# A sliding-window copy: half-size staging transfers, a first batch half loaded in two channel parts, and a first tile filled in two channel ranges

## The chip, the cores and the metric

The kernel runs on one core of a Trainium2 chip. The metric is device time in microseconds for one execution; the median of three runs of the kernel before is 185.81 us (185.74 to 185.81).

## The reference

The input `x` has 16 batches, 64 channels and 64 x 64 pixels, all float32 (16.78 MB). The output has, for each batch and each of 15 x 15 window places, all 64 channels of an 8 x 8 window; windows step by 4, so neighbours overlap by half. Nothing is calculated:

```python
for i in range(n_h):
    for j in range(n_w):
        result[:, i, j] = x[:, :, 4*i:4*i+8, 4*j:4*j+8]
```

The output is 3600 rows of 4096 floats (16 KB each, 58.98 MB). So each input pixel is read once and written nearly four times.

## The kernel before, in words

**Layout.** The image is cut in height into four quarters of 16 rows (`HQ`), the channels into two halves of 32 (`CH`, here ch0 and ch1), the batch into two halves of eight (`NY`, here y=0 and y=1). The tile `Lt` holds the whole input: a partition is one (channel half, batch, height quarter), with 32 channels of 16 x 64 pixels. ch0 sits on partitions 0 to 63, ch1 on 64 to 127, and in each the first 32 partitions are y=0.

**Two ways in.** The first eight channels of each half (`FC` = 8) are *staged*: eight transfers of 512 KB (L118, four on ScalarE's queue, four on SyncE's) put them into the output buffers `GG`, which are not in use yet, and 16 copies (L137, n % 3 == 0 on ScalarE, the others on VectorE) bring them to `Lt`. A staging transfer writes 16 partitions, and reads DRAM in pieces of 4 KB (one channel, 16 rows). The other 24 channels of each half go straight into `Lt` (L61, called at L126 to L128): for each y and height quarter q, SyncE loads 22 channels of ch0 (for the first six of the eight (y, q) cut in two transfers of 10 and 12), GpSimd (POOL) loads the remaining two channels of ch0 (64 KB) and then all 24 of ch1 (768 KB). Each direct load writes eight partitions. ScalarE and SyncE together have eight transfers in flight before an issue waits for an earlier one to land, and POOL has eight of its own: the ninth and later issues each carry a wait on the semaphore of the transfer eight before.

**Tiles out.** `GG` is four output buffers (`G[0]` to `G[3]`) of 128 partitions x 16 KB. There are 31 tiles. A tile is filled by copies out of `Lt` and then stored; tile n goes into buffer n % 4, so its fill waits until tile n-4 has been stored. Stores of the first 29 tiles are indirect transfers from POOL (L149), behind POOL's loads in the same queue; the last two are issued by SyncE (L258). I number the tiles from 0.

- Tiles 0, 1 and 2 are `part(0, j)` (L200): eight copies of 32 partitions x 2048 elements (L208; n % 3 == 0 on ScalarE, the others on VectorE). They need y=0 alone.
- Then `unit(j, 0)` (64-partition copies, L169) and `part(1, j)` alternate: tiles 3 to 8. They need y=1 too. Tile 4 and tile 8 are both `part(1, j)` in `G[0]`.
- Tiles 9 to 28 are mostly "cross" units, three for each plain one; in these VectorE does two plain shuffles (L179) and two shifting shuffles (L172). A cross tile has 112 rows to store.
- The last two tiles (L256) are the last window column.

Order on each engine is the order of the program: all copies out of the staging first, then tile 0, 1, and so on.

Of the kernel before, what the change touches and what calls it, by code (L numbers as in the profile page):

```python
# [10 lines left out]
def kernel(  # L11
# [7 lines left out]
    nc = tc.nc  # L19
    P = nc.NUM_PARTITIONS  # L20

    B, C, H, W = x.shape
    Bo, NH, NW, Co, WSo, WSo2 = out.shape
    WS = int(window_size)
    ST = int(stride)
# [5 lines left out]
    CH = 2  # L31
    HQ = P // (B * CH)
    CL = C // CH
# [6 lines left out]
    NY = B // YB  # L40
    QP = YB * HQ
# [10 lines left out]
    L = Lt[:, :, 0 : RB * W].rearrange("p c (r w) -> p c r w", r=RB)  # L52
# [1 line left out]

    SMALL, SPLIT = 2, 6

    def load(eng, ch, y, q, c0, c1):
        p0 = ch * HP + y * QP + q  # L60
        eng.dma_start(out=L[p0 : p0 + QP - HQ + 1 : HQ, c0:c1, :, :], in_=x_v[ch, y, q, :, c0:c1, :])  # L61
# [49 lines left out]
    TC = GF // (RB * W)  # L111
    FC = NG * TC // CH
    S = [GG[:, ch * NG // CH : (ch + 1) * NG // CH].rearrange("p n f -> p (n f)").rearrange("p (c r w) -> p c r w", c=FC, r=RB) for ch in range(CH)]
    x_b = x.rearrange("b (ch cl) (hq r) w -> ch hq b cl (r w)", ch=CH, hq=HQ)
    for q in range(HQ):
        for ch in range(CH):
            s = S[ch][QP + q : QP + q + (B - 1) * HQ + 1 : HQ]
            (nc.scalar, nc.sync)[ch].dma_start(out=s, in_=x_b[ch, q, :, 0:FC, :])  # L118

    for y in range(NY):
        for q in range(HQ):
            mid = (FC + CL) // 2
            for c0, c1 in [(FC + SMALL, mid), (mid, CL)] if y * HQ + q < SPLIT else [(FC + SMALL, CL)]:
                load(nc.sync, 0, y, q, c0, c1)  # L126
            load(nc.gpsimd, 0, y, q, FC, FC + SMALL)
            load(nc.gpsimd, 1, y, q, FC, CL)  # L128

    PC = TC // 2  # L130
    first = [(0, ch, c) for ch in range(CH) for c in range(0, FC, PC)]
    then = [(1, ch, c) for ch in range(CH) for c in range(0, FC, PC)]
    for n, (y, ch, c) in enumerate(first + then):
        f = slice(QP + y * QP, QP + (y + 1) * QP)
        d = slice(ch * HP + y * QP, ch * HP + (y + 1) * QP)
        copy = nc.vector.tensor_copy if n % 3 else nc.scalar.copy
        tc.keep_in_program_order(copy(out=L[d, c : c + PC, :, :], in_=S[ch][f, c : c + PC]))  # L137
# [10 lines left out]
    def scatter(g, ix, j, s):  # L148
        st = nc.gpsimd.indirect_dma_start(  # L149
            out=o_v,  # L150
            out_offset=bass.IndirectOffsetOnAxis(ap=ix[:, 0:1], axis=0),
            in_=g.rearrange("p c r w -> p (c r w)"),
            in_offset=None,
            element_offset=(s * NW + j) * CFREE,
            bounds_check=B * NWIN - 1,
            oob_is_err=False,
        )
        free(st)
# [36 lines left out]
    def tile_():  # L195
        nonlocal at
        at += 1
        return G[(at - 1) % NG]

    def part(y, j):  # L200
        g = tile_()
        order = [(d, ch) for ch in range(CH) for d in range(P // QP)]
        for n, (d, ch) in enumerate(order):
            s, dj = d // NY, d % NY
            cols = slice((j + dj) * ST, (j + dj) * ST + WS)
            f = (ch * NY + y) * QP
            tc.keep_in_program_order(
                (act if n % 3 == 0 else dve)(  # L208
                    out=g[d * QP : (d + 1) * QP, ch * CL : (ch + 1) * CL, :, :],
                    in_=L[f : f + QP, :, s * ST : s * ST + WS, cols],  # L210
                )
            )
        scatter(g, (idx_y0, idx_y1)[y], j, 0)
# [16 lines left out]
            scatter(g, (idx_hi, idx_lo)[turn], j, s)  # L230

    for n in range(EARLY):
        part(0, 2 * n)
    plain = [(j, 0) for j in range(2 * EARLY, NW - 1)]
    cross = [(j, 2) for j in range(NW)]
    for n in range(EARLY):
        unit(*plain.pop(0), (dve, dve))
        part(1, 2 * n)
# [8 lines left out]
    j = NW - 1  # L247
    for s in range(2):
        g = tile_()
        cols = slice(j * ST, j * ST + WS)  # L250
        for y in range(NY):
            d = slice(QP + y * QP, QP + (y + 1) * QP)
            for ch in range(CH):
                f = slice(ch * HP + y * QP, ch * HP + (y + 1) * QP)
# [39 lines left out]
```

## Time and profile before

| | us |
|---|---|
| median of three runs | 185.81 |
| the profiled execution | 185.77 |
| its span, first to last instruction | 184.0 |
| outside the span | 1.77 |
| VectorE busy (DVE) | 153.9 (84%) |
| ScalarE busy (ACT) | 150.6 (82%) |
| GpSimd busy (POOL) | 49.6 (27%) |
| first copy out of the staging | 17.6 |
| first copy of tile 0 | 29.9 |
| first store issued | 36.95 |
| last copy ends | 173.7 |

A window row gives a stretch of the span, its length, then each engine's busy time with the number of instructions, the granted clock, and last the mean busy share of the 16 DMA engines and the rate they moved. The share can be a little above 1, since a packet may begin before the one ahead of it on the same engine has ended. In a timeline row the first number is the start, the second the time from the start of the first instruction merged into the row to the end of the last, and the bracket at its end says how long the engine had been idle and what ended that.

### The profile page before, as it was taken

How to read it: one execution, taken by the hardware profiler on the slowest of the kernel's cores; microseconds unless marked ns; L12 is line 12 of the kernel's file. 1: busy time of each engine (PE TensorE's matmuls, PEld its weight loads, DVE VectorE, ACT ScalarE, POOL GpSimd, SP SyncE). 2: the span in 40 equal slices, each digit the busy share in tenths (PEclk: the TensorE clock that was granted, in tenths of full speed). 3: DMA queues.
4: the chain of work that ended last, by engine and by line, in shares of the span. 5: the costliest groups of instructions: out<-in, count | busy, mean ns of one | idle time of the engine just before them, and what ended most of it. 6: DMA issues, size and time to landing. Idle time of an engine off the chain costs nothing.

```text
span 184.0 us, 612 instructions
## 1 busy us (share of the span) xinstructions
DVE 153.9 (84%) x213; ACT 150.6 (82%) x100; POOL 49.6 (27%) x50
## 2 busy tenths in 40 slices
DVE  5001999999999897999999999999999999999700
ACT  0001999999999999999899999998979999899600
POOL 7500575033253434221121112111211121113000
DMA  5999999999999999999999999999999999999995
GB/s 157 398 411 407 411 412 409 413 410 444 422 431 435 424 442 417 447 424 431 431 426 435 427 438 427 431 424 431 422 420 427 427 427 403 435 417 406 420 431 232
DMA packets 10596, 75.80 MB, mean 412 GB/s; under 512 B 2896, under 2 KB 2896, under 8 KB 6992
## 3 DMA queue, kind: packets, MB, share of 16 engines
q0 software_dynamic: 7760, 63.71, 82.4%
q1 hardware_dynamic: 2256, 9.96, 13.3%
q10 hardware_dynamic: 576, 2.10, 3.1%
q14 instruction: 4, 0.03, 0.0%
HBM read 16.78 MB, written 62.91 MB: 433 GB/s over the span
## 4 chain that ended last, share of the span: by engine, by line
DVE 61%; DMA 21%; issue 10%; SPq 1%; DVEq 1%
DVE GG L179 24%; DVE GG L172 16%; DVE GG L208 15%; DMA GG<-in_x_dram 8%; DMA out_dram<-GG,idx_y 7%; DMA Lt<-in_x_dram 6%; DVE GG L256 3%; DVE GG L169 2%; SPq L118 1%; DVE GG L184 0%; DVEq L289 0%; DVEq L169 0%; DVEq L208 0%; DVEq L179 0%; DVEq L256 0%
## 5 line engine op out<-in xcount | busy, mean ns | idle before, releaser
L169 ACT COPY GG<-Lt 64x2048 f32<-64x2048 f32 x46 | 87.2, 1897 | 3.9 <-DMA out_dram<-GG,idx 1.2
L179 DVE STREAM_SHUFFLE GG<-Lt 64x1024 f32<-64x1024 f32 (+4 forms) x39 | 52.9, 1357 | 1.3
L208 DVE COPY GG<-Lt 32x2048 f32<-32x2048 f32 x30 | 36.6, 1218 | 2.7 <-DMA out_dram<-GG,idx_y 1.6
L172 DVE STREAM_SHUFFLE GG<-Lt 64x1024 f32<-64x1024 f32 x30 | 38.5, 1282 | 0.0
L208 ACT COPY GG<-Lt 32x2048 f32<-32x2048 f32 x18 | 34.1, 1897 | 0.4
L137 DVE COPY Lt<-GG 32x2048 f32<-32x2048 f32 x10 | 11.8, 1224 | 14.1 <-DMA GG<-in_x_dram 14.0
L61 POOL DMA_DIRECT2D Lt<-in_x_dram x16 | 14.1, 886 | 16.3 <-DMA Lt<-in_x_dram 15.7
L149 POOL DMA_INDIRECT out_dram<-GG,idx_y x6 | 10.1, 1690 | 27.6 <-DVE GG L208 27.6
L149 POOL DMA_INDIRECT out_dram<-GG,idx_lo x8 | 7.7, 966 | 30.2 <-DVE GG L172 18.9
L137 ACT ACT_TABLE_LOAD x1 | 1.3, 1283 | 17.6 <-DMA GG<-in_x_dram 17.6
L149 POOL DMA_INDIRECT out_dram<-GG,idx x8 | 10.6, 1321 | 18.1 <-DVE GG L179 13.3
L149 POOL DMA_INDIRECT out_dram<-GG,idx_hi x7 | 6.8, 966 | 26.5 <-DVE GG L172 18.9
L137 ACT COPY Lt<-GG 32x2048 f32<-32x2048 f32 x6 | 11.2, 1894 | 0.1
L183 ACT COPY GG<-Lt 64x256 f32<-64x256 f32 (+2 forms) x21 | 10.2, 484 | 0.5
L169 DVE COPY GG<-Lt 64x2048 f32<-64x2048 f32 x6 | 7.3, 1222 | 0.2
L256 ACT COPY GG<-Lt 32x768 f32<-32x768 f32 x8 | 6.6, 828 | 0.1
L256 DVE COPY GG<-Lt 32x1280 f32<-32x1280 f32 x8 | 6.5, 818 | 0.1
L75 DVE TENSOR_SCALAR tb<-pi 128x1 int32<-128x1 int32 x1 | 0.2, 154 | 1.0 <-POOL pi L72 1.0
L184 DVE COPY GG<-Lt 64x1280 f32<-64x1280 f32 x1 | 0.9, 875 | 0.0
L78 DVE TENSOR_SCALAR th<-tc 128x1 int32<-128x1 int32 x2 | 0.3, 154 | 0.0
L81 DVE TENSOR_TENSOR th<-tc,tq 128x1 int32<-128x1 int32 x2 | 0.3, 154 | 0.0
L179 DVE LOAD_MASK_SELECT GG<-Lt x39 | 0.3, 7 | 0.0
(21 smaller groups left out, 3.0 us busy)
## 6 DMA issues: line engine op xcount, KB each, us to landing
Lt<-in_x_dram POOLq DMA_DIRECT2D x8, 768.0 KB, 15.7
Lt<-in_x_dram SPq DMA_DIRECT2D x6, 384.0 KB
GG<-in_x_dram SPq DMA_DIRECT2D x4, 512.0 KB
GG<-in_x_dram ACTq DMA_DIRECT2D x4, 512.0 KB
out_dram<-GG SPq DMA_DIRECT2D x2, 1024.0 KB
Lt<-in_x_dram SPq DMA_DIRECT2D x6, 320.0 KB
Lt<-in_x_dram SPq DMA_DIRECT2D x2, 704.0 KB
Lt<-in_x_dram POOLq DMA_DIRECT2D x8, 64.0 KB, 15.2
```

The source lines that it names most:

```text
L61: eng.dma_start(out=L[p0 : p0 + QP - HQ + 1 : HQ, c0:c1, :, :], in_=x_v[ch, y, q, :, c0:c1, :])
L78: nc.vector.tensor_scalar(out=d[:, :], in0=a[:, :], scalar1=float(m), scalar2=None, op0=ALU.mult)
L118: (nc.scalar, nc.sync)[ch].dma_start(out=s, in_=x_b[ch, q, :, 0:FC, :])
L137: tc.keep_in_program_order(copy(out=L[d, c : c + PC, :, :], in_=S[ch][f, c : c + PC]))
L149: st = nc.gpsimd.indirect_dma_start(out=o_v, out_offset=bass.IndirectOffsetOnAxis(ap=ix[:, 0:1], axis=0), in_=g.rearrange("p c r w -> p (c ...
L169: copy(out=g[d, cs, :, :], in_=L[f, :, s * ST : s * ST + WS, cols])
L172: nc.vector.stream_shuffle(out=g[d, cs, ST:WS, :], in_=L[f, :, 0:ST, cols], mask=nxt)
L179: nc.vector.stream_shuffle(out=out, in_=in_, mask=same)
L183: act(out=out[:, 0:k], in_=in_[:, 0:k])
L184: other(out=out[:, k:], in_=in_[:, k:])
L208: (act if n % 3 == 0 else dve)(out=g[d * QP : (d + 1) * QP, ch * CL : (ch + 1) * CL, :, :], in_=L[f : f + QP, :, s * ST : s * ST + WS, cols],)
L256: copy(out=g[d, ch * CL + c0 : ch * CL + c1, :, :], in_=L[f, c0:c1, s * ST : s * ST + WS, cols])
```

## The change

The staging goes in two rounds of four channels: sixteen transfers of 256 KB in place of eight of 512 KB. The copies out of it are the same sixteen, in another order: first all of channels 0 to 3 (both y, both halves), then 4 to 7.

The direct loads of y=0 are cut at channel 20 (`MID`): first channels 8 to 19 for all four q, then 20 to 31 for all four q, then y=1 as before. In each of the three blocks POOL again loads two channels of ch0 and all of ch1, so it issues 24 loads in place of 16. SyncE still issues 14: 10 channels, 10 channels, and for y=1 the first two q cut in 10 and 12, the others whole.

Tile 0 is filled in two channel ranges, 0 to 19 for all eight partition pieces and then 20 to 31, in 16 copies in place of 8. All other tiles are as before.

```diff
-    SMALL, SPLIT = 2, 6
+    SMALL, SPLIT, MID = 2, 2, 20
...
-    for q in range(HQ):
-        for ch in range(CH):
-            s = S[ch][QP + q : QP + q + (B - 1) * HQ + 1 : HQ]
-            (nc.scalar, nc.sync)[ch].dma_start(out=s, in_=x_b[ch, q, :, 0:FC, :])
-    for y in range(NY):
+    for c in range(0, FC, TC):
         for q in range(HQ):
-            mid = (FC + CL) // 2
-            for c0, c1 in [(FC + SMALL, mid), (mid, CL)] if y * HQ + q < SPLIT else [(FC + SMALL, CL)]:
-                load(nc.sync, 0, y, q, c0, c1)
-            load(nc.gpsimd, 0, y, q, FC, FC + SMALL)
-            load(nc.gpsimd, 1, y, q, FC, CL)
+            for ch in range(CH):
+                s = S[ch][QP + q : QP + q + (B - 1) * HQ + 1 : HQ, c : c + TC]
+                (nc.scalar, nc.sync)[ch].dma_start(out=s, in_=x_b[ch, q, :, c : c + TC, :])
+    for y, c0, c1 in ((0, FC, MID), (0, MID, CL), (1, FC, CL)):
+        for q in range(HQ):
+            mid = (c0 + c1) // 2
+            for a, b in [(c0 + SMALL, mid), (mid, c1)] if y and q < SPLIT else [(c0 + SMALL, c1)]:
+                load(nc.sync, 0, y, q, a, b)
+            load(nc.gpsimd, 0, y, q, c0, c0 + SMALL)
+            load(nc.gpsimd, 1, y, q, c0, c1)
...
-    first = [(0, ch, c) for ch in range(CH) for c in range(0, FC, PC)]
-    then = [(1, ch, c) for ch in range(CH) for c in range(0, FC, PC)]
-    for n, (y, ch, c) in enumerate(first + then):
+    moves = [(y, ch, c + n) for c in range(0, FC, TC) for y in range(NY) for ch in range(CH) for n in range(0, TC, PC)]
+    for n, (y, ch, c) in enumerate(moves):
...
-    def part(y, j):
+    def part(y, j, ranges=((0, CL),)):
         g = tile_()
-        order = [(d, ch) for ch in range(CH) for d in range(P // QP)]
-        for n, (d, ch) in enumerate(order):
+        order = [(d, ch, c0, c1) for c0, c1 in ranges for ch in range(CH) for d in range(P // QP)]
+        for n, (d, ch, c0, c1) in enumerate(order):
...
-                    out=g[d * QP : (d + 1) * QP, ch * CL : (ch + 1) * CL, :, :],
-                    in_=L[f : f + QP, :, s * ST : s * ST + WS, cols],
+                    out=g[d * QP : (d + 1) * QP, ch * CL + c0 : ch * CL + c1, :, :],
+                    in_=L[f : f + QP, c0:c1, s * ST : s * ST + WS, cols],
...
-        part(0, 2 * n)
+        part(0, 2 * n, *([] if n else [((0, MID), (MID, CL))]))
```

## The prediction

> **What bounds the kernel now.** I read the page's slices first, then its queue lines, then a table of stretches, then the chain of waits, then the timeline of the engine that the chain names.
>
> The slices:
>
> ```profile
> DVE  5001999999999897999999999999999999999700
> ACT  0001999999999999999899999998979999899600
> POOL 7500575033253434221121112111211121113000
> DMA  5999999999999999999999999999999999999995
> ```
>
> Two things look full: the DMA engines from the first slice on, and VectorE (DVE) with ScalarE (ACT) from the fourth. Only one can be what the end waits for.
>
> ```profile
> core 0: us, DVE busy (x) ACT busy (x) POOL busy (x), PEclk, DMA share, GB/s
> 2.00:6.00 4.00, 1.42 (x11) 0.00 (x0) 4.00 (x8) 1.00 0.95 306
> 6.00:17.00 11.00, 0.00 (x0) 0.00 (x0) 0.94 (x2) 1.00 1.03 411
> 17.00:44.00 27.00, 25.61 (x22) 26.11 (x15) 11.32 (x9) 1.00 1.04 412
> 70.00:130.00 60.00, 58.93 (x88) 57.87 (x41) 13.53 (x13) 1.00 1.01 431
> 130.00:174.00 44.00, 43.06 (x64) 40.98 (x33) 8.76 (x9) 1.00 1.00 420
> 174.00:182.00 8.00, 0.00 (x0) 0.00 (x0) 0.00 (x0) 1.00 0.99 422
> ```
>
> From 6 to 17 us VectorE and ScalarE do nothing, and the DMA share is 1.03 all the same: the DMA engines don't miss them. From 17 to 44 it is 1.04, and after that about 1.0. So the transfers run back to back from 2.2 us (the first packet) to 182.2 (the last).
>
> ```profile
> DMA packets 10596, 75.80 MB, mean 412 GB/s; under 512 B 2896, under 2 KB 2896, under 8 KB 6992
> ## 3 DMA queue, kind: packets, MB, share of 16 engines
> q0 software_dynamic: 7760, 63.71, 82.4%
> q1 hardware_dynamic: 2256, 9.96, 13.3%
> q10 hardware_dynamic: 576, 2.10, 3.1%
> ```
>
> 82.4 + 13.3 + 3.1 = 98.8% of 184.0 us is 181.8 us of packet time on each of 16 engines, in a stretch of 180.0 us (packets overlap by about 1%). **The DMA work is the time.** By the trace's packet records a packet of 16 KB takes 611 to 616 ns, one of 4 KB 159, one of four bytes (a semaphore count or a filler) 9. The page gives 2896 of the last, 6992 - 2896 = 4096 of 4 KB (the input once) and 3604 larger ones, 3600 of them output rows.
>
> Is VectorE bound too? The chain and the timeline around 70 us answer:
>
> ```profile
> 58.06 11.98 DMA out_dram<-GG,idx_y
> 70.05 0.03 issue
> 70.09 0.04 issue
> 70.14 1.23 DVE GG L208
> ```
>
> ```profile
> 70.14 6.22 DVE L208 COPY GG<-Lt 32x2048 f32<-32x2048 f32 x5 [0.94 <-DMA out_dram<-GG,idx_y]
> ```
>
> VectorE stands still for 0.66 us up to 60.47 (tile 6) and, as this row shows, for 0.94 up to 70.14 (tile 8) until buffers are stored, the second time until tile 4's store, issued at 58.06, has landed at 70.05. That store waited in the queue behind tiles 0 to 3. So tile 8 begins when the DMA engines have finished all loads and five tiles, and nothing done earlier on VectorE moves that. From there VectorE has no further stop of note (58.93 of 60.00 us) and is a little slower than the stores: a cross tile is issued every 4.74 us and its 112 rows take 4.26 us. Its lead, from the end of an issue to the tile's first packet, falls from 5.2 us (tile 7) to 1.25 (tile 27). That is why the rate sinks from 431 to 420 GB/s after 130 us.
>
> **The change, part by part**, against the profiled execution (185.77 us, 0.04 under the median).
>
> *Bytes and large packets:* the same. Every channel still comes in 4 KB pieces: 4096 x 159 ns stay.
>
> *More transfers.* The page's 576 packets on q10 are four staging transfers of 128 pieces and 16 counts each. A SyncE direct load posts eight counts (2256 = 4 x 144 + 1408 pieces + 14 x 8 + two stores of 64 + 16): it runs on eight engines of the 16. A POOL load puts pieces on eight engines, a filler for each on the other eight, and 16 counts; with 16 counts for each of 29 stores and 240 skipped rows that gives the 2624 four-byte packets of q0. From 20 to 40 us q1 takes 7.4 engines (46.3% of 16) and q0 9.2: **SyncE's ch0 fills one half of the engines, POOL's ch1 the other.** Added now: 8 staging transfers x 16 counts = 128; 8 POOL loads x 16 counts = 128; 64 fillers for the eight more 64 KB loads. On an engine of the ch0 half that is 8 + 8 = 16 packets, on the other 8 + 8 + 8 = 24: 16 x 9 = 0.14 us and 24 x 9 = 0.22 us. The ch0 half is the later one (its loads end at 44.4 us, the other's at 43.9, and first stores start on the other at 43.2), so I take **+0.13 us**, bounds 0 (counts run beside data) and +0.22. The 64 fillers stay inside it.
>
> The Trainium skill (SBUF — State Buffer, The DMA setup-cost knee) gives every transfer a fixed cost of about 2 us, mostly completion, and speaks against this change. As an estimate by that page, 16 more transfers one after the other would be 32 us, to 218. The 1.03 from 6 to 17 us, under eight staging transfers and a queue behind each, shows such a cost hidden while the next transfer is queued.
>
> *The start.* From 2 to 6 us 306 GB/s x 4 us = 1.22 MB are moved, where 411 GB/s would be 1.64: 1.0 us is lost there, while the first transfers ramp up. With 256 KB each, the first eight hold 2.1 MB, about 5 us of work, and SyncE and ScalarE issue one each 0.6 to 0.8 us (L118: 3.06 us for four), which supplies 0.5 MB in 0.75 us, above what the engines take. The ninth waits for the first to land; six or seven are then still queued, so I take 0, bounds -0.3 (shorter first transfers land their data sooner) and +1.0 (the loss doubles with the number of hand-overs).
>
> *Copies out of the staging* begin when 2.1 MB instead of 4.2 have landed, at about 9 to 10 us instead of 17.6, and end near 22. *Tile 0* still needs the last y=0 loads of ch1, which now land near 30 (27.9 before: they queue behind more), so its store can go out near 33 instead of 36.95; the eight extra copies are smaller, 16 x 32 partitions, some 60 ns more each, all in front of a wait. *Tile 3* needs all loads, near 44.5. All this is **time at no price and no gain**: the first store's packets can't run before the loads are through (43.2 us now, 4.5 us after its issue ended), and tile 8 waits for tile 4's store as shown. Without the cover: tile 3 later than 56 us would stop the DMA; it is about 49.
>
> Sum: 185.77 + 0.13 + 0 = **185.90 us**.
>
> **Rivals.**
>
> *POOL can't feed its half (slower).* This is the mechanism of the other sign.
>
> ```profile
> 1.48 4.92 POOL L61 DMA_DIRECT2D Lt<-in_x_dram  x8 [0.52 <-issue]
> ...
> 22.22 2.76 POOL L61 DMA_DIRECT2D Lt<-in_x_dram  x2 [2.00 <-DMA Lt<-in_x_dram]
> ```
>
> Eight issues took 4.92 us before VectorE copied, 0.62 each; beside its copies a pair took 2.76, 1.38 each. Copies now start at 9.5 us, and 16 of the 24 loads fall beside them, so nearly all late issues are of the slow kind. A pair of 64 + 384 KB gives the ch1 half 384 KB / 206 GB/s = 1.9 us of work and costs POOL up to 2.8. Four such pairs must follow the first four: 4 x 0.9 = 3.6 us short. Against it: three pairs, 5.7 us, are queued when a wait ends, and the ch1 half is 1.2 us ahead. It decides once issue plus the way to the first packet passes 5.7 us: that way was at most 1.25 us at tile 27 (4.0 in all, safe) and 3.4 at the very first POOL load (6.2, not safe). Price: 3.6 - 1.2 = 2.4 at the worst, half of it likely: 187.1, from 186.2 to 188.3. The Trainium skill (SBUF — State Buffer, SBUF: two separate sides) says GpSimd can't write descriptors while VectorE copies float32 in its two-port mode; the rise from 0.62 to 1.38 agrees with it.
>
> *The start loses more (slower).* Twice as many hand-overs between short transfers: +0.4 to +1.0, 186.3 to 186.8. A fixed cost per transfer, as on the page named above, would show itself here.
>
> *The lead is larger to the end (faster).* Tiles 0 to 2 are filled some 4 us sooner. If that lead lived on, the 52 us after 130 us would run at 431 instead of 420 GB/s: 52 x 11/431 = 1.3 us, 184.6; half of it, 185.3. Against it stand the two stops at 60.47 and 70.14: a lead is taken back there.
>
> *It doesn't do what it says:* if the copies start no sooner (the second round of staging holds ScalarE's queue), the time is that of the main case, by the same argument.
>
> **How the numbers follow.** 0.2% is 0.37 us, about what a measurement of this kernel can tell from no change; "same" reaches from 185.44 to 186.18. Main case 0.57 (185.6 to 186.15), POOL's half 0.17, start 0.13, lead 0.10, something not seen on the slow side 0.03. The faster cases come to 0.11, the slower ones to 0.32 (a little of each lies inside the bound), same 0.57. The range reaches from half of the lead case to the middle of POOL's: 185.3 to 187.2.
>
> **What would show it.** Right: DMA share near 1.03 from 6 to 44 us with SyncE's and POOL's queues both full, copies from about 9.5 us, the stops of VectorE at tiles 6 and 8 longer than 0.66 and 0.94, tile 8 again beginning at 70.1 to 70.3, the rate after 130 us again near 420. POOL's rival: a stretch between 22 and 32 us with a share near 0.5 to 0.8. The start's: 2 to 6 us with less than 1.2 MB. The lead's: VectorE waiting for buffers after 80 us and 430 GB/s to the end. Wrong altogether if tile 4's store lands more than 0.4 us from 70.05 with the DMA share full, since then the packets themselves cost something else.

## The result, and the profile after

The changed kernel takes 187.13 us, median of six runs (186.87 to 187.52), beside 185.78 (185.68 to 185.83) for the kernel before: a ratio of 1.0072, 95% interval 1.0059 to 1.0085. That is 1.35 us, or 0.72%, slower. The profiled execution also took 187.13, with a span of 185.3 us (184.0 before). The time lies in the range given, at its upper end (187.2); the main case, 185.90, was 1.2 us too low.

The table of stretches of the kernel after, with the columns that the prediction showed:

```profile
2.00:6.00 4.00, 1.43 (x11) 0.00 (x0) 4.00 (x8) 1.00 0.94 295
6.00:17.00 11.00, 5.19 (x5) 4.71 (x3) 3.08 (x4) 1.00 0.99 364
17.00:44.00 27.00, 23.31 (x24) 23.99 (x17) 15.84 (x15) 1.00 1.03 410
70.00:130.00 60.00, 58.12 (x88) 57.17 (x39) 13.91 (x14) 1.00 1.01 430
130.00:174.00 44.00, 43.31 (x65) 41.76 (x35) 9.24 (x10) 1.00 1.00 422
```

Row by row against before: 6 to 17 us fell from 411 to 364 GB/s, which is 47 x 11 = 517 KB, or 1.26 us at 411. The rows on each side lost 11 x 4 KB and 2 x 27 KB, 0.1 us each. After the loads the rates are those of before (430 for 431, 422 for 420). So the load phase lost 1.5 us, and 0.2 came back at the end. The busy share hides this: it reads 0.99, and only the rate tells. In single microseconds:

```profile
6.00:7.00 1.00, 0.00 (x0) 0.00 (x0) 0.75 (x2) 1.00 0.68 258
...
8.00:9.00 1.00, 0.00 (x0) 0.00 (x0) 0.00 (x0) 1.00 0.97 320
...
15.00:16.00 1.00, 1.00 (x2) 0.99 (x2) 0.54 (x1) 1.00 1.19 352
16.00:17.00 1.00, 0.99 (x2) 1.00 (x1) 0.00 (x0) 1.00 0.72 287
```

These rows count a packet, with its whole time and bytes, in the microsecond in which it starts: the 0.68 at 6 us and the 0.72 at 16 are low for the most part because packets of over 1 us, begun in the microsecond before, still run (by the time that packets run, the engines are 0.94 and 0.96 busy there; the 1.19 at 15 us holds five such packets). Taken apart, the packet records show two kinds of loss. Some packets take long: 90 of 4 KB took over 220 ns (up to 1.5 us) where the kernel before has 54, 76 of the 90 on ScalarE's and SyncE's queues; together they ran 27.9 us beyond 159 ns each (12.2 before). And some engines have nothing to do: idle engine time from 2 to 46 us, added up over the 16 engines, is 13.6 us (6.0 before), of it 10.2 up to 6 us and 3.2 from 6 to 17 (5.95 and none before). (27.9 - 12.2) / 16 = 1.0 us and (13.6 - 6.0) / 16 = 0.5 us, together the same loss from the other side. Two thirds of it is long packets.

What the two issuing queues did, ScalarE's and SyncE's rows of the timeline, after:

```profile
0.74 11.50 ACTq L119 DMA_DIRECT2D GG<-in_x_dram  x8
0.74 11.65 SPq L119 DMA_DIRECT2D GG<-in_x_dram  x8
13.42 7.12 SPq L61 DMA_DIRECT2D Lt<-in_x_dram  x8
```

and before:

```profile
0.74 2.60 ACTq L118 DMA_DIRECT2D GG<-in_x_dram  x4
0.74 3.06 SPq L118 DMA_DIRECT2D GG<-in_x_dram  x4
4.75 15.72 SPq L61 DMA_DIRECT2D Lt<-in_x_dram  x10
```

Before, all staging was issued by 3.8 us and direct loads followed from 4.75. After, the second round's issues waited one by one (ScalarE's began at 4.07, 6.25, 9.61 and 11.67, SyncE's at 4.66, 6.88, 9.79 and 11.84), and the first direct load on SyncE came at 13.42.

What the loss did further on, VectorE's rows of the timeline after:

```profile
11.77 6.04 DVE L138 COPY Lt<-GG 32x2048 f32<-32x2048 f32 x5 [8.12 <-DMA GG<-in_x_dram]
19.25 6.10 DVE L138 COPY Lt<-GG 32x2048 f32<-32x2048 f32 x5 [1.44 <-DMA GG<-in_x_dram]
...
31.28 15.33 DVE L209 COPY GG<-Lt 32x768 f32<-32x768 f32 x15 [1.72 <-DMA Lt<-in_x_dram]
...
71.28 3.71 DVE L209 COPY GG<-Lt 32x2048 f32<-32x2048 f32 x3 [0.97 <-DMA out_dram<-GG,idx_y]
```

The copies begin at 11.77 (17.6 before), tile 0's first range is done early, and its second waits for the last y=0 loads until 31.28. The first store is issued at 35.02 instead of 36.95, but its first packet starts at 44.65 instead of 43.23, 1.42 later. Tile 8 begins at 71.28 instead of 70.14, 1.14 later, released as before by tile 4's store. The span ends 1.3 later: little is added on the way from there to the end.

### The profile page after: what moved, and what is told of

Read it like the earlier page. It is cut to its first block, busy times and chain, and to the rows that moved or that the text cites. A ratio compares the mean times of both kernels' runs of the same rounds, so it can differ in the third digit from the quotient of the medians.

```text
span 185.3 us, 651 instructions
## 1 busy us (share of the span) xinstructions
DVE 154.9 (84%) x218; ACT 151.4 (82%) x103; POOL 55.8 (30%) x58
## 2 busy tenths in 40 slices
DMA packets 10916, 75.81 MB, mean 409 GB/s; under 512 B 3216, under 2 KB 3216, under 8 KB 7312
## 4 chain that ended last, share of the span: by engine, by line
DVE 45%; DMA 38%; issue 9%; SPq 1%; ACTq 1%; DVEq 1%
DVE GG L180 20%; DMA out_dram<-GG,idx_y 16%; DVE GG L173 14%; DMA GG<-in_x_dram 9%; DMA Lt<-in_x_dram 7%; DVE GG L209 6%; DMA out_dram<-GG,idx_hi 6%; DVE GG L257 3%; SPq L61 1%; ACTq L119 1%; DVEq L290 1%; DVE GG L185 0%; DVE GG L170 0%; DVEq L209 0%; DVEq L180 0%
## 5 line engine op out<-in xcount | busy, mean ns | idle before, releaser
L209 DVE COPY GG<-Lt 32x2048 f32<-32x2048 f32 (+2 forms) x35 | 37.3, 1067 | 6.5 <-DMA out_dram<-GG,idx_y 3.9
L209 ACT COPY GG<-Lt 32x2048 f32<-32x2048 f32 (+2 forms) x21 | 34.7, 1653 | 4.0 <-DMA Lt<-in_x_dram 2.7
L61 POOL DMA_DIRECT2D Lt<-in_x_dram x24 | 19.8, 836 | 12.4 <-DMA Lt<-in_x_dram 11.5
L150 POOL DMA_INDIRECT out_dram<-GG,idx x8 | 11.6, 1445 | 19.4 <-DVE GG L180 9.9
L184 ACT COPY GG<-Lt 64x256 f32<-64x256 f32 (+2 forms) x21 | 10.2, 484 | 0.5
## 6 DMA issues: line engine op xcount, KB each, us to landing
Lt<-in_x_dram POOLq DMA_DIRECT2D x8, 384.0 KB, 11.1
```

The costliest lines, as they stand in the source:

```text
L150: st = nc.gpsimd.indirect_dma_start(out=o_v, out_offset=bass.IndirectOffsetOnAxis(ap=ix[:, 0:1], axis=0), in_=g.rearrange("p c r w -> p (c ...
L184: act(out=out[:, 0:k], in_=in_[:, 0:k])
L209: (act if n % 3 == 0 else dve)(out=g[d * QP : (d + 1) * QP, ch * CL + c0 : ch * CL + c1, :, :], in_=L[f : f + QP, c0:c1, s * ST : s * ST + ...
```

## The experiments

**Theory:** the time went because smaller staging transfers leave fewer bytes under way. ScalarE and SyncE have eight transfers in flight together: 8 x 512 KB = 4.2 MB before, 8 x 256 KB = 2.1 MB after. **Rivals:** the loads in parts (POOL can't feed its half), the early copies disturbing the transfers, tile 0's ranges, and a price per transfer whatever its size.

All kernels below take part in one table (S: staging in halves, P: loads in parts, R: ranges of tile 0):

| kernel | S | P | R | us | ratio to before, 95% interval |
|---|---|---|---|---|---|
| before | | | | 185.8 | |
| e1 | x | | | 193.17 | 1.0395 [1.0376, 1.0414] |
| e2 (copy order of before) | | x | | 185.80 | 1.0003 [0.9994, 1.0012] |
| e5 | | x | | 185.76 | 1.0004 [0.9995, 1.0013] |
| e6 | | | x | 186.12 | 1.0013 [1.0004, 1.0022] |
| e3 | x | x | | 187.40 | 1.0099 [1.0082, 1.0116] |
| e4 | | x | x | 186.50 | 1.0034 [1.0021, 1.0047] |
| after | x | x | x | 187.13 | 1.0072 [1.0059, 1.0085] |

### One part at a time: staging, loads

The kernel before with the staging in two rounds and the new order of its copies alone:

```diff
-            s = S[ch][QP + q : QP + q + (B - 1) * HQ + 1 : HQ]
-            (nc.scalar, nc.sync)[ch].dma_start(out=s, in_=x_b[ch, q, :, 0:FC, :])
+    for c in range(0, FC, TC):
...
+                s = S[ch][QP + q : QP + q + (B - 1) * HQ + 1 : HQ, c : c + TC]
+                (nc.scalar, nc.sync)[ch].dma_start(out=s, in_=x_b[ch, q, :, c : c + TC, :])
...
-    for n, (y, ch, c) in enumerate(first + then):
+    moves = [(y, ch, c + n) for c in range(0, FC, TC) for y in range(NY) for ch in range(CH) for n in range(0, TC, PC)]
+    for n, (y, ch, c) in enumerate(moves):
```

> The kernel before with the staging in two rounds of 256 KB transfers and the copies in the new order; direct loads and tile 0 as before. Start theory (the half-size staging transfers leave the DMA engines short between 2 and 17 us): 186.8 to 187.2, with about 364 GB/s from 6 to 17 us. POOL theory (the 24 loads issued beside copies cost the time): 185.8 to 186.0, with 411 GB/s from 6 to 17 us.

And the kernel before with the direct loads of y=0 in two parts alone:

```diff
-    SMALL, SPLIT = 2, 6
+    SMALL, SPLIT, MID = 2, 2, 20
...
-    for y in range(NY):
+    for y, c0, c1 in ((0, FC, MID), (0, MID, CL), (1, FC, CL)):
```

> The kernel before with the direct loads of y=0 in two channel parts (24 POOL loads); staging, copies and tile 0 as before. Start theory: 185.8 to 186.1, 411 GB/s from 6 to 17 us. POOL theory: 186.8 to 187.2, a dip between 22 and 32 us.

The staging alone takes 193.17, five times the whole change's loss; the loads in parts alone take 185.80, nothing. So the cause is in the staging, and POOL's rival is out: e2 has all of POOL's 24 issues, and its dip, at 28 to 30 us, where the direct loads of y=0 give way to y=1, is small:

```profile
27.00:28.00 1.00, 1.00 (x2) 1.00 (x2) 1.00 (x2) 1.00 1.03 414
28.00:29.00 1.00, 0.81 (x1) 1.00 (x1) 1.00 (x1) 1.00 1.11 340
29.00:30.00 1.00, 0.44 (x1) 0.97 (x2) 1.00 (x3) 1.00 0.89 340
```

That the staging alone costs so much more than the whole change was not foreseen. Its stretches:

```profile
6.00:17.00 11.00, 5.95 (x5) 5.46 (x4) 0.94 (x2) 1.00 1.02 382
17.00:44.00 27.00, 18.24 (x16) 19.50 (x11) 7.51 (x8) 1.00 1.04 416
44.00:70.00 26.00, 18.86 (x16) 17.73 (x10) 6.58 (x4) 1.00 0.82 348
```

The start loses (411 - 382) x 11 = 0.32 MB, 0.8 us, less than in the kernel after. Most of the rest goes at 44 to 70 us, (432 - 348) x 26 = 2.2 MB, 5 us; from 70 to 130 us another 1.5 (420 for 431 GB/s). In the timeline there:

```profile
56.89 3.82 ACT L170 COPY GG<-Lt 64x2048 f32<-64x2048 f32 x2 [8.07 <-DMA Lt<-in_x_dram]
56.91 2.47 DVE L170 COPY GG<-Lt 64x2048 f32<-64x2048 f32 x2 [6.68 <-DMA Lt<-in_x_dram]
```

Tile 3, the first that needs all loads, waits until 56.9 us for one (48.57 was its start before), and the page's rate shows the hole behind it, in slices of 4.8 us: 435, 430, **144, 277**, 440. That a load should land at 56 us, 12 us later than in the kernel before, needed a second theory.

### Do stores overtake loads?

**Second theory.** An engine of the ch0 half has SyncE's queue with loads and POOL's queue, where each ch1 piece has left a filler of four bytes. The queues take turns packet by packet. Normally POOL's stores come behind fillers that last as long as the loads. If SyncE's queue runs dry for a moment, the fillers go through without loads beside them (in e1, POOL's queue passed 133, 275 and 131 four-byte packets in the three microseconds from 11 us on; by 42 to 44 us only 5 are left to pass, where the kernel before still passes 103 then and 78 from 44 to 46), and later the stores get to the ch0 engines while loads are still there. A load of 4 KB then gets one turn for each store packet of 611 ns. The packet records of e1 agree, in mean engines busy and packets of 4 KB and more started in 2 us (some rows left out):

```
us          loads (SyncE's queue)     POOL's queue
42 to 44    6.87 engines, 81 packets   9.47 engines, 103
46 to 48    1.33,         17          14.79,          45 (611 ns each)
52 to 54    0.24,          3          15.88,          52
56 to 58    0.08,          1          16.02,          51
58 to 60    0                          8.88,          23
60 to 62    0                          0.53,           1
```

From 50 us two or three loads of 4 KB pass in 2 us: one engine, taking turns with 611 ns. The Trainium skill (DMA: Bandwidth & Descriptors, Queues, rings and completion order) says that each engine goes round its queue rows packet by packet; this table agrees.

**Test.** If it is so, e1 must lose almost nothing when no store can be issued before the loads are through. `EARLY = 0` does that: no tile is then filled from y=0 alone (the output is the same, the tiles come in another order). It was put on the kernel before and on e1:

```diff
-    EARLY = 3
+    EARLY = 0
```

> The kernel before, with EARLY = 0: no tile is filled from y=0 alone, the first tile needs all loads, so no store can be issued before the loads are through. All theories: later than 185.8, since the first store now comes only after about 44 us plus a fill of some 4 to 5 us (about 48 to 50 us in place of 43.2 for the first packet): 190 to 193. This is the base for the next kernel; the two are compared with each other.

> The kernel with the staging in two rounds (193.17 with its early tiles) and EARLY = 0. Overtaking (my theory): no store is in the queue while ch0's loads still come, so the last SyncE load ends near 46 us and not near 56, and this kernel is only the start's loss, 1 to 2 us, behind the one with EARLY = 0 and whole staging: 191 to 195. Rival (the 7.4 us are lost in the load phase itself, by the small transfers): it is again about 7 us behind that kernel, 197 to 200, with the last load near 50 us or later.

Measured: 204.59 (204.53 to 204.63) and 205.51 (205.3 to 206.02). Both are far above my 190 to 195, since with this order the first store is issued only at 57.59 and 59.05 us: ScalarE first runs eight 64-partition copies. But the comparison that the runs were for is clear: **the halves cost 0.9 us here, not 7.4.** ScalarE's row where the last load has landed, before with EARLY = 0:

```profile
45.31 15.20 ACT L169 COPY GG<-Lt 64x2048 f32<-64x2048 f32 x8 [13.43 <-DMA Lt<-in_x_dram]
```

and e1 with EARLY = 0:

```profile
46.77 15.20 ACT L170 COPY GG<-Lt 64x2048 f32<-64x2048 f32 x8 [20.18 <-DMA Lt<-in_x_dram]
```

46.77 - 45.31 = 1.46 us: this is what the halves lose in the load phase, with no tile, store or range in play, and it agrees with the kernel after's 1.42. SyncE's last load ends at 46.0 there, and at 56.2 in e1, whose loads and staging are the same: without early stores the loads aren't late, so stores that overtake loads are shown. That they get ahead because the fillers have passed is read from the packet counts; no run tried it. The order with `EARLY = 0` costs 204.59 - 185.81 = 18.8 us in all: without the first three tiles the DMA engines stand empty from 44.6 to 59.2.

### The change without ranges, and with whole staging

The kernel after, tile 0 in one range:

```diff
-        part(0, 2 * n, *([] if n else [((0, MID), (MID, CL))]))
+        part(0, 2 * n)
```

> The kernel after, with tile 0 filled in one range (8 copies). Both theories: 187.0 to 187.3, as the kernel after, since tile 0's fill has 7 us to spare. If splitting tile 0 itself costs or saves something, it shows as a difference from 187.13 beyond 0.3.

The kernel after, its staging in eight transfers of 512 KB again:

```diff
-    for c in range(0, FC, TC):
...
-                s = S[ch][QP + q : QP + q + (B - 1) * HQ + 1 : HQ, c : c + TC]
-                (nc.scalar, nc.sync)[ch].dma_start(out=s, in_=x_b[ch, q, :, c : c + TC, :])
+            s = S[ch][QP + q : QP + q + (B - 1) * HQ + 1 : HQ]
+            (nc.scalar, nc.sync)[ch].dma_start(out=s, in_=x_b[ch, q, :, 0:FC, :])
```

> The kernel after with its staging back at eight transfers of 512 KB, everything else as after (loads in parts, copies in the new order, tile 0 in two ranges). Start theory: 185.8 to 186.1, 411 GB/s from 6 to 17 us. POOL theory: 187.0 to 187.3.

Measured: 187.40 (187.01 to 188.26) and 186.50 (186.08 to 186.64). e3 against e1 differs in the loads in parts alone, and takes 5.8 us less: they hide most of what the halves do. In the kernel after POOL's first loads hold 12 channels instead of 24, so fewer fillers are queued when SyncE's queue is short (242 four-byte packets in the microsecond from 12 us on, beside 20 and 17 in its neighbours), and SyncE's and POOL's loads both end near 46 us, before the stores spread. That this is why was read from the traces alone. e3 also shows the scatter of a single profile: with the staging and loads of the kernel after it moved 384 GB/s from 6 to 17 us, not 364. SyncE's last load ends at 46.2 us in both (44.6 in the kernel before).

With whole staging the row of the start is back, in e4:

```profile
6.00:17.00 11.00, 0.37 (x1) 0.41 (x1) 1.87 (x4) 1.00 1.03 412
```

So the halves make the hole at 6 to 17 us. But e4 is 0.7 us above the kernel before, which I had not expected, and its loads show no reason: tile 8 begins at 70.15. Two kernels looked for it: e4 with tile 0 in one range (e3's edit on it), and the kernel before with the ranges alone:

```diff
-    def part(y, j):
+    def part(y, j, ranges=((0, CL),)):
...
-        part(0, 2 * n)
+        part(0, 2 * n, *([] if n else [((0, MID), (MID, CL))]))
```

> The changed kernel with the staging back to eight transfers of 512 KB and tile 0 in one range. If the 0.7 us that the changed kernel with whole staging takes over the kernel before come with tile 0's ranges: 185.7 to 185.9. If they come with the new order of the copies out of the staging together with the loads in parts: 186.3 to 186.7.

> The kernel before with tile 0 alone filled in two channel ranges (0 to 19, then 20 to 31), staging and loads as before. If the ranges themselves cost the 0.7 us by which whole staging with loads in parts and ranges (186.50) stands above the same without ranges (185.76): 186.3 to 186.7. If the ranges cost nothing by themselves, and the 0.7 us come only together with loads in parts, or from run to run: 185.6 to 186.0.

Measured: 185.76 (185.59 to 186.26), so the 0.7 goes with the ranges; and 186.12 (185.93 to 186.34), so the ranges by themselves cost 0.24 us, interval 0.07 to 0.41. In e6 VectorE's tiles 0 to 2 take 19.52 us instead of 18.66, the first store is issued 0.64 later, and tile 8 begins 0.50 later. Whether that is how they cost it isn't shown: e6's profile has 286 GB/s from 2 to 6 us (306 before), 0.2 us lost long before tile 0 is filled. The other half us of e4 is not explained. In its profile all 16 engines work to 182.1 us, and one alone goes on from 182.4 to 183.2 (0.4 us of this is in the kernel before too); why that engine has more to do isn't known. In the kernel after the ranges cost nothing (187.13 with, 187.40 without, intervals overlapping): the tiles wait for late loads there.

### Bytes in flight, or number of transfers?

Three kernels change the bytes under way or the size of a transfer, each otherwise.

*Fewer bytes, same staging transfers:* the kernel before, with an unused transfer of 64 bytes for each staging transfer. Nothing else is changed; the tiny ones take half of the eight places, so 4 x 512 KB = 2.1 MB are under way.

```diff
+            t = ipool.tile([1, 16], f32, name=f"tiny{q}{ch}")
+            (nc.scalar, nc.sync)[ch].dma_start(out=t[:, :], in_=x_b[ch, q, 0:1, 0, 0:16])
```

> The kernel before; behind each pair of 512 KB staging transfers SyncE and ScalarE also issue one transfer of 64 bytes each into an unused tile. The eight places in flight are then half taken by these, so only four staging transfers (2.1 MB) can be in flight, as with eight of 256 KB, while their shape and the copies stay. Theory 'bytes in flight' (halving the transfers halved what may be in flight, and engines that carry no POOL load run out while the others still work): 186.8 or more, up to 193 as with the staging change alone, less than 400 GB/s from 6 to 17 us. Rival 'shape' (four pieces per partition are slower to move than eight): 185.8 to 186.2.

*A quarter of the bytes:* the kernel after, staging in four rounds of 128 KB (1.05 MB under way).

```diff
-    for c in range(0, FC, TC):
+    for c in range(0, FC, PC):
```

> The kernel after with the staging in four rounds of 128 KB transfers (32 of them), the copies in the order of after. Bytes in flight: eight now hold 1.05 MB, 2.6 us of work; at least another 2.5 us on top of after: 189.5 to 195. Shape: also slower, 188 to 190. Cost per transfer alone (a count on each engine): 16 x 9 ns more, 187.1 to 187.5.

*Twice the size:* the kernel before, four staging transfers of 1 MB, both channel halves in one (`SS` is `S` of both halves in one view).

```diff
-        for ch in range(CH):
...
-            (nc.scalar, nc.sync)[ch].dma_start(out=s, in_=x_b[ch, q, :, 0:FC, :])
+            s = SS[QP + q : QP + q + (B - 1) * HQ + 1 : HQ, :, c : c + FC, :]
+            (nc.scalar, nc.sync)[q % 2].dma_start(out=s, in_=x_m[q, :, :, c : c + FC, :])
```

> The kernel before with both channel halves of a quarter staged by one transfer: four of 1 MB in place of eight of 512 KB, two on each queue. Bytes in flight: no wait of SyncE's loads for a place until four more are issued, so the start can only fill better: 185.3 to 185.8. If the 1.0 us lost before 6 us is the ramp of the first packets alone: 185.7 to 185.9.

Measured: 190.19 (189.42 to 190.8), ratio 1.0235 [1.0214, 1.0257]; 205.66 (205.36 to 205.85), 1.1067 [1.105, 1.1084]; 185.98 (185.89 to 186.28), 1.0015 [1.0006, 1.0024]. The first lies where it was expected; the second is far above what was expected, the third a little above. From their stretches; g2, with the size of the staging transfers unchanged:

```profile
6.00:17.00 11.00, 0.00 (x0) 0.00 (x0) 1.03 (x3) 1.00 0.97 359
```

f3, in four rounds:

```profile
2.00:6.00 4.00, 1.43 (x11) 0.00 (x0) 4.00 (x8) 1.00 0.80 249
6.00:17.00 11.00, 1.34 (x2) 0.00 (x0) 2.98 (x6) 1.00 1.00 328
```

f4, twice the size:

```profile
6.00:17.00 11.00, 0.00 (x0) 0.00 (x0) 0.93 (x2) 1.00 1.03 411
```

g2 has the kernel after's hole (359 beside 364 GB/s) with transfers of 512 KB and no copies in the way: the size of a transfer isn't what costs. It too loses more later (401 from 44 to 70 us, SyncE's last load at 53.7), as e1 does; that e1 takes 3 us more than g2 is not explained. g2 has eight transfers more than the kernel before, as the halves have, so by itself it doesn't tell bytes from a price per transfer. Such a price doesn't fit the other runs: eight more on POOL's queue cost nothing (e2, e5), four fewer in f4 bring no gain, and sixteen more in f3 cost 18.5 us where the first eight cost 1.6 (e3 beside e5). In f3 the rate sinks with the bytes, and the later loss is larger (tile 3's ScalarE copies wait 15.45 us for a load, to 69.70). Twice the size, with the bytes under way no less, gains nothing. The Trainium skill (DMA: Bandwidth & Descriptors, Measured) has a rule to batch transfers to 1 MiB or more for at least 75% of the peak; here 512 KB and 1 MB transfers both move 411 GB/s from 6 to 17 us, so that rule doesn't decide this stage.

*Early copies:* the kernel before, its staging transfers reordered, first the four of ch0 and then the four of ch1, each set spread over both queues; the copies follow in that order and begin at 11.1 us.

```diff
-    for q in range(HQ):
-        for ch in range(CH):
+    for ch in range(CH):
+        for q in range(HQ):
...
-            (nc.scalar, nc.sync)[ch].dma_start(...)
+            (nc.scalar, nc.sync)[q % 2].dma_start(...)
```

> The kernel before; the eight 512 KB staging transfers in another order, first the four of ch0, then the four of ch1, each set on both queues, and the copies in that order, so that copies start some 6 us sooner, without more transfers. Bytes in flight, and shape: 185.7 to 186.1. Rival 'early copies' (VectorE's copies beside POOL's load issues cost the time): 187 or more.

Measured: 185.71 (185.63 to 185.8), ratio 0.9998 [0.9989, 1.0007].

```profile
6.00:17.00 11.00, 5.84 (x5) 5.92 (x4) 0.95 (x2) 1.00 1.03 412
```

VectorE and ScalarE work 5.84 and 5.92 us in this stretch, more than in the kernel after (5.19 and 4.71), and the rate stays at 412: the copies disturb nothing. They bring nothing either, as the prediction said. No kernel here beats the kernel before.

**What makes a place come free late.** A staging transfer spans all 16 engines, and its sixteen semaphore counts come in two groups. ScalarE's third in the kernel after, issued at 2.07 us, had eight counts by 7.7 us and the other eight from 8.6 to 9.6; its place was taken again at 9.61. I read the late eight as the ch1 half, where POOL's loads stand beside the staging as a third queue, and suppose that the ch0 half has by then run through what the eight places hold for it. The records don't name the engine of a packet, and from 7 to 15 us they show only 0.2 us of idle engine time but 38 long packets. So this is not shown, and no run tried it by itself.

## Why the prediction was right or wrong

**Failed: the start.** "The ninth waits for the first to land; six or seven are then still queued, so I take 0, bounds -0.3 [...] and +1.0." This step took 2.1 MB under way to be enough because several transfers would still be queued. It isn't: the places came free one at a time, 2.1 to 3.4 us apart on each queue, and 2.1 MB in transfers of 512 KB (g2) leave the same hole. The term is +1.4 us (1.42 at the first store's packet, 1.46 between the two kernels without early stores), above its upper bound. How too few bytes become lost time is known in part: a third of it is engines with nothing to do, two thirds are long packets, whose cause stays open. My test for it looked at 2 to 6 us and less than 1.2 MB, and can't tell: the kernel after had 295 x 4 = 1.18 MB there, but e3, with halves too, had 1.28, and e6, with whole staging, 1.14. Most of the loss came later, with the long packets at 5 to 10.5 and 15 to 17 us. The rival "the start loses more" named this with 0.4 to 1.0 us: right in its place, too small, and its reason, a price for each hand-over, doesn't fit the runs together. The copies out of the staging began at 11.77 us, not at 9 to 10.

**Right: DMA work sets the time,** and in the kernel after the delay of the loads goes to the end nearly unshortened: 1.42 at the first store, 1.14 at tile 8, 1.3 at the span.

**Right: an early first store brings nothing.** It was issued 1.93 us sooner (I said near 33 us, it was 35.02) and its packets came later. h1 shows the same with copies from 11.1 us.

**Right: the buffers' waits.** Tiles 6 and 8 waited 0.92 and 0.97 us (0.66 and 0.94 before), tile 8 again for tile 4's store. But that the store landed more than 0.4 us from 70.05 with the DMA share full was my sign for "wrong altogether", since the packets themselves would then cost something else. It came, and it fits: the shift is that of the load phase, where the share read 0.99 and most of the loss was in packets of 4 KB that took longer than the 159 ns of the sum.

**Count right, price not measurable:** the page after counts 3216 packets under 512 B, the 320 more that were worked out. e2 and e5 have 192 of them (3088) and take 185.80 and 185.76.

**Wrong, small: tile 0's ranges** were put down as free, "all in front of a wait". By themselves they cost 0.24 us; how isn't shown.

**POOL's rival** had the measured time, 187.1, by chance. Its mechanism isn't in the trace: in the kernel after POOL waited 11.5 us in its loads for transfers to land, so it was not the late one; e2 and e5 keep its issues and lose nothing. So it is luck too that the time lies in the range: this rival set the upper end, 187.2, while the main case ended at 186.15 and the start's rival at 186.8. **The lead's rival** gave 422 for 420 GB/s after 130 us, 0.2 us.

## What to carry to other kernels

Where a fixed number of transfers may be in flight, cutting transfers in half halves the bytes under way; before doing so, work out whether what is left lasts until the slowest engine has landed its part of the oldest transfer (the counts of ScalarE's third transfer came over a stretch of 2.8 us). Where loads and stores share engines by turns, a short gap in the loads can cost several times its length (e1: 1.46 us of load time lost without early stores, 7.4 us of the kernel's time with them), because a store packet is nearly four times as long as a load packet (611 and 159 ns). Read the rate beside the busy share: 0.99 stood over a loss of 11%.

## What had not been expected of the hardware

- Half the bytes in flight cost 1.4 us of load time; the stores that overtook the loads made that 7.4 us (e1), until the loads were cut in parts (e3, 187.40).
- With a quarter of the bytes in flight, 1.05 MB, the kernel took 205.66 us (187.13 with half): the loss grows much faster than the bytes shrink.
- Packets of 4 KB that mostly take 159 ns took up to 1.5 us, most of them on ScalarE's and SyncE's queues, at the times when these were refilled (5 to 10.5 and 15 to 17 us in the kernel after); they are counted as busy, and are two thirds of what the load phase lost. Why they are so long stays open.
